# Weight tiles kept together on TensorE: k, r and v in groups of four tiles, and the decay's and a's products after the keys

## The chip, the cores and the metric

The kernel runs on one core of one Trainium2 chip. The metric is the device time of one execution in microseconds (us); lower is better. Before the change three runs took 1529.62, 1530.75 and 1531.14 us.

## The reference

One inference step of a decoder trunk with two layers, on 256 prompt tokens and 8 x 4 sample tokens (288 columns in all), everything in float32 with a model width of 1024. Cut to what matters:

```python
def trunk(x, p, ssm0, conv0, wkv0, shift0, prm):
    h = x
    for i in range(DEPTH):                      # 2 layers
        h = h + 0.5 * swiglu(rmsnorm(h, ...), ...)
        u = rmsnorm(h, ...)
        mix = mamba2_mixer(u, ...) if i % 2 == 0 else rwkv7_mixer(u, ...)
        h = h + mix
        h = h + 0.5 * swiglu(rmsnorm(h, ...), ...)
        h = h + (p[i] @ ple_in[i]) * sigmoid(rmsnorm(h, ...) @ ple_gate[i])
    return rmsnorm(h, norm_final), states

def rwkv7_mixer(u, S0, shift0, ...):
    # six mixtures of u with its predecessor: xr, xw, xk, xv, xa, xg
    r, k, v = xr @ w_r, xk @ w_k, xv @ w_v
    w = -softplus(-(w0 + tanh(xw @ w1) @ w2)) - 0.5          # the decay
    a = sigmoid(a0 + (xa @ a1) @ a2)
    g = sigmoid(xg @ g1) @ g2
    # per head of 64: kk = normalised k * k_k;  k = k * (1 + (a - 1) * k_a)
    # per token: S = S * exp(-exp(w)) - (S kk) (kk a)^T + v k^T ;  y = S r
    return (groupnorm(y) + bonus) * g @ w_o
```

## The kernel before, in words

All activations lie with features on the 128 partitions and the 288 tokens along the free dimension. A weight matrix is cut into tiles of 128 x 128. Most products run in three passes, so that a fast matmul format keeps float32 precision: a weight tile is split into a high part `whi` (by ScalarE, L57) and a low part `wlo` (by VectorE, L58), the activation is split in the same way, and `mm3` (L156) issues high x high, high x low and low x high into the same bank of PSUM. The key projection is the exception: it goes in plain float32 on the unsplit tile `raw` (`next_whole`, L71; the profile shows two matmul records for one such tile). Every matmul is issued by `mm` (L147), so most of them stand in the profile under line 149. Weight tiles come in the order of use from one packed stream (`Stream`, L28), eight tiles a transfer, split four tiles at a time.

The program is written with a tile framework that schedules when the kernel is built: it walks through the program with its own estimate of time, and whenever an engine is free it gives it, among the instructions whose inputs are ready, the one that comes first in program order. What it decides is then fixed: on the chip each engine runs its instructions strictly in that order and waits on semaphores. `high_priority()` is a block of the framework; instructions traced in it stand ahead of all others in this choice as soon as they are ready. `add_manual_dep` (in `after`, L127) fixes an order by hand; `mm` uses it only while `kept` is set, at the end of the RWKV stage.

The stages follow each other: feed-forward, Mamba, feed-forward, gated embedding, feed-forward, RWKV, feed-forward, gated embedding. The change concerns above all the RWKV stage (`rwkv`, L1516). It works on eight head pairs p = 0 to 7 of 128 features each. For a head pair there are three kinds of work:

- *bulk*: the projections. `bulk` (L1155) makes, for p > 0, first the products of the decay and of a (`small`, L1166: two matmuls each, then `sigmoid`, L1130, one VectorE and three ScalarE steps), then k (L1175), then r; `bulk2` (L1181) makes g and v. `proj` (L1138) takes eight weight tiles for k, r or v and yields after each. For p = 0 it also makes the mixtures of the activations (`mix`, L1115), and `small` comes after k.
- *prep* (L1234): from k, r, the decay and a of the head pair it makes the per-chunk matrices and inverts a triangular one by doubling; many matmuls on 64 x 64 quarters of the array, each followed by a ScalarE or VectorE step that the next one needs.
- *chain* (L1384): the recurrence over four chunks of 64 tokens and the samples: `solve`, `solved` and `state` for each chunk, again small matmuls with a step of another engine in between, then the group norm.

The loop at L1565 writes these in program order: in one round the chain of pair p-2, the second half of the preparation of p-1 and the first half of that of p advance by one step each, and then the bulk by 1.6 steps (`RATE`). `fill(p)` (L1545) says which bulk belongs to round p: g and v of p-1, then the decay, a, k and r of p+1. The banks of PSUM are dealt out in rings (L1527): the bulk has two in turn, the preparation three, the chain two and one for its outputs. `d["sw"]` and `d["sa"]` (the decay and a) have one buffer each, `d["k"]`, `d["r"]`, `d["v"]` and `d["g"]` two.

Of the kernel before, what the change touches and what calls it, by code (L numbers as in the profile page):

```python
# [1 line left out]

# [16 lines left out]
KD = 8  # L19
# [61 lines left out]
class K:  # L81
# [71 lines left out]
            self.kept = [i]  # L153
        return i

    def mm3(self, ps, w, x, start, stop):  # L156
        (wh, wl), (xh, xl) = w, x
        self.mm(ps, wh, xh, start=start, stop=False)
        self.mm(ps, wh, xl, start=False, stop=False)
        self.mm(ps, wl, xh, start=False, stop=stop)  # L160

    def hilo(self, hi, lo, src, scale=None):

# [686 lines left out]
def mamba(k, gain, g_next):  # L850
# [8 lines left out]

    with k.tc.tile_pool(name="mamba", bufs=1) as pool:  # L860
        pdt = proj("m_dt", 0)
        r = k.rstd()
        k.other = True
# [30 lines left out]
        for g in range(8):  # L894
            if g == 1:
                k.set_rings(main=[0, 1, 2], aux=[3, 4, 5, 6, 7])
            tiles = [("c", 16 + g), ("c", 24 + g), ("c", 2 * g), ("c", 2 * g + 1), ("z", 0), ("z", 1)]
            for n, (kind, i) in enumerate(tiles):
                if g == 0 and n == RAW:
                    k.flip()  # L900
                ps = proj("m_xbc" if kind == "c" else "m_z", i if kind == "c" else 2 * g + i)

                def evac(ps=ps, kind=kind, i=i, g=g, n=n, raw=g == 0 and n < RAW):
                    if kind == "c":
                        conv.setdefault(g, []).append(m.conv(g, n, i, ps, raw))
                    else:
                        t = m.t("z", bufs=3)
                        k.act(t, ps, AF.Copy)
                        zl.append((g, i, t))

                k.lag(evac)
                step()
                if n == 0 and g > 0:
                    boundary(g - 1)
                    gen = m.ssd(g - 1)
                if g == 0 and n in (0, 1):
                    next(dtg, None)
                if n > 0 and ahead is not None:
                    next(ahead, None)
                if g % 2 == 1 and g > 1 and n in (1, 2):  # L920
                    (m.norm_act, m.norm_dve)[n - 1](g - 2)
# [85 lines left out]
class Rwkv:  # L1007
# [130 lines left out]
    def proj(self, n, i, x, p):  # L1138

        k, d = self.k, self.d[p]  # L1140
        ps = k.bank("main")[:, :NT]
        for kt in range(KD):
            if p == 0:
                self.mix(i, kt, x)
            if n == "k":
                self.k.mm(ps, k.wn.next_whole("r_wk", kt, p), x[kt], start=kt == 0, stop=kt == KD - 1)
            else:
                k.mm3(ps, k.ws.next("r_w" + n, kt, p), x[kt], kt == 0, kt == KD - 1)
            if kt < KD - 1:
                yield  # L1150
        d[n] = self.t(n, bufs=2)
        k.act(d[n], ps, AF.Copy)
        yield

    def bulk(self, p):  # L1155

        nc, k = self.nc, self.k
        col = slice(p, p + 1)
        if p == 0:
            k.renew(0, 8, F32)  # L1160
            k.renew(8, 16)
            self.xk = k.A[0:8]
            self.xv, self.xr = [[None] * KD for _ in range(2)]
        d = self.d[p] = {}

        def small():  # L1166
            for n, x, b in (("sw", self.lw, "w0"), ("sa", self.la, "a0")):
                ps = k.bank("main")[:, :NT]
                self.stacked(ps, k.ws.next("r_" + n[1] + "2", 0, p), x)
                d[n] = self.t(n)  # L1170
                self.sigmoid(d[n], ps, k.g(b)[:, col])
            yield

        if p > 0:
            yield from small()  # L1175
        yield from self.proj("k", 2, self.xk, p)
        if p == 0:
            yield from small()
        yield from self.proj("r", 0, self.xr, p)

    def bulk2(self, p):  # L1181
# [334 lines left out]
def rwkv(k, g, g_next):  # L1516
# [3 lines left out]
    with k.tc.tile_pool(name="rwkv", bufs=1) as pool:  # L1520
# [44 lines left out]
        for p in range(KD + 2):  # L1565
            gens, acc = [], 0.0
            bulk = fill(p)
            if p > 1:
                gens.append(w.chain(p - 2))
            if 0 < p <= KD:  # L1570
                gens.append(preps.pop(p - 1))
            if p < KD:
                preps[p] = w.prep(p)
                gens.append(itertools.islice(preps[p], HALF))
            while gens:
                for q in list(gens):
                    if next(q, "end") == "end":
                        gens.remove(q)
                if w.last:
                    k.kept = k.kept or []  # L1580
                    acc += w.last.pop(0)
                else:
                    acc += RATE
                while acc >= 1:
                    acc -= 1
                    next(bulk, None)
            for _ in bulk:
                pass
# [198 lines left out]
```

## Time and profile before

| | us |
|---|---|
| median of three runs | 1530.75 |
| lowest and highest | 1529.62, 1531.14 |
| the profiled execution | 1529.38 |
| its span, first to last instruction | 1527.6 |
| one feed-forward stretch, 600 to 700 us: matmuls | 759 |
| RWKV's head pairs, 1003 to 1269 us: matmuls | 3971 |

How to read it: PE is TensorE's matmuls, PEld its weight loads, which overlap them; DVE is VectorE, ACT ScalarE, POOL GpSimd, SP the engine that issues the transfers. A line of the timeline gives start, length, engine, line, operation, what it writes and reads, the used part of the array (rows\*columns), the shape of the moving operand and how many of the kind stand together; a bracket at its end tells how long the engine was idle before it and who released it. A matmul's own length overlaps that of its neighbours, so differences of starts tell what it occupies. `bank<-act,whi` is a pass on the high part of a weight tile, `act,wlo` on the low part, `act,raw` the key projection, `lw` and `la` the products of the decay and a, `lgh`, `lgl` and `lg` those of g; names such as `X,N`, `Z,XT`, `rhs,TT` or `SAV,BKt` are the small matmuls of preparation and chain.

### The profile page before, as it was taken

What the parts mean: (1) busy time and instruction counts of PE and PEld (TensorE: products, weight loads), DVE (VectorE), ACT (ScalarE), POOL (GpSimd) and SP (SyncE); (2) the same over time, 40 slices, a digit from 0 to 9 for tenths busy, and PEclk for the clock granted to TensorE, in tenths of its full rate; (3) what the DMA queues carried; (4) which work ended last, traced back from release to release, by engine and by line L of the source; (5) the groups of instructions that cost most, each with busy time, mean ns of one, the idle gap of its engine ahead of it and who ended that gap; (6) DMA issues with size and microseconds to landing.
All of it is one profiled execution on the core that took longest, in us unless ns stands there. A gap on an engine that the chain in (4) does not pass through costs nothing.

```text
span 1527.6 us, 35589 instructions
## 1 busy us (share of the span) xinstructions
PE 1504.1 (98%) x14178; PEld 1418.5 (93%) x14178; DVE 1099.2 (72%) x2320; ACT 966.1 (63%) x2201; POOL 60.2 (4%) x162
## 2 busy tenths in 40 slices
PE   9999999999999999999999999999999999999997
PEld 9999998999999999999999999777777778999997
DVE  7666578899998666656876655897777768666666
ACT  6555458999997655554755554586666646555545
POOL 0000002112110000000000000200000000000000
PEclk9999999999999999999999999999999999999999
DMA  7555564766766555555555555622221125555552
GB/s 233 166 167 165 167 204 138 241 235 214 240 220 195 174 167 167 165 169 166 170 166 166 166 166 166 208 84 73 71 85 58 62 75 165 167 167 166 166 169 68
DMA packets 75575, 243.48 MB, mean 159 GB/s; under 512 B 11728, under 2 KB 16976, under 8 KB 75408
## 3 DMA queue, kind: packets, MB, share of 16 engines
q1 hardware_dynamic: 75408, 241.21, 49.1%
q8 instruction: 111, 1.82, 0.5%
q14 instruction: 56, 0.46, 0.1%
HBM read 226.54 MB, written 14.64 MB: 158 GB/s over the span
## 4 chain that ended last, share of the span: by engine, by line
PE 91%; DVE 4%; ACT 3%; DMA 1%; issue 1%; SPq 0%; DVEq 0%; ACTq 0%
PE bank L149 85%; PE bank L783 1%; DVE wlo L58 1%; PE bank L787 1%; PE bank L779 1%; DMA raw<-in_wn 1%; ACT whi L57 1%; PE bank L760 0%; DVE AA L1288 0%; ACT L136 0%; PE bank L818 0%; ACT seg L141 0%; DMA raw<-in_w 0%; PE bank L752 0%; ACT xc L141 0%
## 5 line engine op out<-in xcount | busy, mean ns | idle before, releaser
L149 PE MATMUL bank<-act,whi 128*128 128x288 f32 x5520 | 1121.7, 297 | 2.5 <-ACT whi L57 1.6
L149 PEld LDWEIGHTS bank<-act,whi 128*128 128x128 f32 x5520 | 885.7, 188 | 11.0 <-ACT whi L57 2.1
L149 PE MATMUL bank<-act,wlo 128*128 128x288 f32 x2760 | 812.4, 295 | 0.1
L57 ACT ACTIVATE whi<-raw 128x512 fp32r<-128x512 f32 x754 | 473.5, 632 | 445.6 <-PE bank L149 435.3
L58 DVE TENSOR_TENSOR wlo<-raw,whi 128x512 fp32r<-128x512 f32 x754 | 515.8, 689 | 270.2 <-ACT whi L57 241.9
L149 PEld LDWEIGHTS bank<-act,wlo 128*128 128x128 f32 x2760 | 520.4, 189 | 1.9 <-DVE wlo L58 0.3
L149 PE MATMUL bank<-more,whi 128*128 128x288 f32 x384 | 77.1, 295 | 0.0
L149 PEld LDWEIGHTS bank<-more,whi 128*128 128x128 f32 x384 | 61.4, 188 | 0.0
L149 PE MATMUL bank<-act,raw 128*128 128x288 f32 x176 | 54.0, 429 | 2.7 <-DVE sw L1133 1.4
L335 DVE TENSOR_TENSOR u<-bank,s 128x288 f32<-128x288 f32 x88 | 40.2, 456 | 22.8 <-PE bank L149 22.8
L149 PE MATMUL bank<-more,wlo 128*128 128x288 f32 x192 | 56.4, 294 | 0.0
L332 DVE TENSOR_TENSOR t<-bank,rstd 128x288 f32<-128x288 f32 x88 | 39.8, 456 | 22.2 <-PE bank L149 22.1
L684 DVE SCALAR_TENSOR_TENSOR conv_a<-X,vec,conv_a 128x312 f32<-128x312 f32 x96 | 51.0, 535 | 2.4 <-ACT conv_a L141 2.1
L141 ACT ACTIVATE s<-t 128x288 f32<-128x288 f32 x104 | 45.8, 443 | 6.1 <-DVE t L377 4.4
L141 ACT ACTIVATE X<-bank 128x256 f32<-128x256 f32 (+2 forms) x98 | 30.6, 343 | 16.9 <-PE bank L149 16.2
L149 PEld LDWEIGHTS bank<-act,raw 128*128 128x128 f32 x176 | 29.9, 189 | 11.2 <-DVE sw L1133 1.7
L141 ACT ACTIVATE act<-h,vec 128x288 fp32r<-128x288 f32 (+1 forms) x71 | 37.0, 527 | 4.1 <-DMA h<-in_xT 2.9
L149 PEld LDWEIGHTS bank<-more,wlo 128*128 128x128 f32 x192 | 36.2, 189 | 0.0
L136 ACT ACT_TABLE_LOAD x25 | 32.1, 1283 | 1.1 <-PEq L1761 0.7
L170 DVE SCALAR_TENSOR_TENSOR act<-h,vec,act 128x288 fp32r<-128x288 f32 x56 | 28.3, 512 | 5.6 <-ACT act L141 5.6
L181 DVE TENSOR_TENSOR ss<-ss,sq 128x288 f32<-128x288 f32 x62 | 28.0, 452 | 1.9 <-ACT sq L141 1.7
L141 ACT ACTIVATE sq<-h 128x288 f32<-128x288 f32 x63 | 26.9, 431 | 3.8 <-DVE h L381 3.7
(371 smaller groups left out, 1605.4 us busy)
## 6 DMA issues: line engine op xcount, KB each, us to landing
raw<-in_w SPq DMA_DIRECT2D x377, 512.0 KB, 3.6
h0a<-in_ssm_a SPq DMA_DIRECT2D x16, 512.0 KB, 5.8
h0b<-in_ssm_b SPq DMA_DIRECT2D x16, 512.0 KB, 5.4
out_ssm_s<-h0b SPq DMA_DIRECT2D x16, 512.0 KB, 4.4
raw<-in_wn SPq DMA_DIRECT2D x11, 512.0 KB, 4.2
S<-in_wkv_in SPq DMA_DIRECT2D x8, 256.0 KB, 3.0
out_wkv_s<-S SPq DMA_DIRECT2D x8, 256.0 KB, 2.1
h<-in_xT SPq DMA_DIRECT2D x8, 144.0 KB, 4.5
```

Of the source, the lines that this page charges most:

```text
L57: nc.scalar.activation(hi, src, AF.Copy)
L58: nc.vector.tensor_tensor(lo, src, hi.bitcast(F32), ALU.subtract)
L136: load = self.nc.scalar.preload_act_table_set(s)
L141: i = self.nc.scalar.activation(out, in_, func, **kw)
L149: i = self.nc.tensor.matmul(*a, **kw)
L170: nc.vector.scalar_tensor_tensor(lo, src, scale, hi.bitcast(F32), ALU.mult, ALU.subtract)
L181: nc.vector.tensor_tensor(self.ss, self.ss, sq, ALU.add)
L332: nc.vector.tensor_tensor(t, pg, r, ALU.mult)
L335: nc.vector.tensor_tensor(u, pu, s, ALU.mult)
L684: nc.vector.scalar_tensor_tensor(a[:, :312], X[:, t:t + 312], k.g(f"conv_w{t}")[:, ct:ct + 1], a[:, :312], ALU.mult, ALU.add)
L779: nc.tensor.matmul(pyi[q:q + 32, 128 + 4 * b:132 + 4 * b], h0a[:, b, q:q + 32], C[:, 256 + 4 * b:260 + 4 * b], start=True, stop=True)
L783: nc.tensor.matmul(py[64 * hh:64 * hh + 64, o:o + n], xdt[:n, c, 2 * j + hh], Pm[:n, hh, o:o + n], start=True, stop=True)
```

## The change

In `mm3` the second and the third pass of every weight tile are traced in a `high_priority()` block, in all stages; the first pass too where the new argument `follow` is set. `proj` sets it for k, r and v of every head pair but the first, for all tiles but the first and the fifth, and for k it puts its float32 matmul in the same block. So from the first pass of tile 0 or 4 on, the passes of four tiles are the scheduler's first choice one after the other. In `bulk` the products of the decay and a now follow the keys for every head pair, as they did before for the first alone. No instruction is added or dropped.

```diff
+    def together(self, follow):
+
+        return self.tc.high_priority() if follow else contextlib.nullcontext()
+
-    def mm3(self, ps, w, x, start, stop):
+    def mm3(self, ps, w, x, start, stop, follow=False):
         (wh, wl), (xh, xl) = w, x
-        self.mm(ps, wh, xh, start=start, stop=False)
-        self.mm(ps, wh, xl, start=False, stop=False)
-        self.mm(ps, wl, xh, start=False, stop=stop)
+        with self.together(follow):
+            self.mm(ps, wh, xh, start=start, stop=False)
+        with self.together(True):
+            self.mm(ps, wh, xl, start=False, stop=False)
+            self.mm(ps, wl, xh, start=False, stop=stop)
...
             if n == "k":
-                self.k.mm(ps, k.wn.next_whole("r_wk", kt, p), x[kt], start=kt == 0, stop=kt == KD - 1)
+                with k.together(p > 0 and kt % 4 > 0):
+                    self.k.mm(ps, k.wn.next_whole("r_wk", kt, p), x[kt], start=kt == 0, stop=kt == KD - 1)
             else:
-                k.mm3(ps, k.ws.next("r_w" + n, kt, p), x[kt], kt == 0, kt == KD - 1)
+                k.mm3(ps, k.ws.next("r_w" + n, kt, p), x[kt], kt == 0, kt == KD - 1, p > 0 and kt % 4 > 0)
...
-        if p > 0:
-            yield from small()
         yield from self.proj("k", 2, self.xk, p)
-        if p == 0:
-            yield from small()
+        yield from small()
         yield from self.proj("r", 0, self.xr, p)
```

More of the change, by code (lines that the diff above doesn't have):

```diff
@@ L1 @@
+import contextlib
 import itertools
```

## The prediction

> **What bounds the kernel now.** I read the page first, then the busy time of the engines by stretches, then TensorE's timeline inside one stretch.
>
> ```profile
> span 1527.6 us, 35589 instructions
> ...
> PE 1504.1 (98%) x14178; PEld 1418.5 (93%) x14178; DVE 1099.2 (72%) x2320; ACT 966.1 (63%) x2201; POOL 60.2 (4%) x162
> ...
> PE 91%; DVE 4%; ACT 3%; DMA 1%; issue 1%; SPq 0%; DVEq 0%; ACTq 0%
> ```
>
> TensorE is busy for 98% of the span and carries 91% of the chain that ended last. So time can be won only by making TensorE's own sequence shorter, and lost only by putting holes into it. The next view shows what a matmul costs in two stretches.
>
> ```profile
> core 0: us, PE busy (x) PEld busy (x) DVE busy (x) ACT busy (x) POOL busy (x), PEclk, DMA share, GB/s
> 600.00:700.00 100.00, 100.00 (x759) 100.00 (x758) 60.26 (x104) 53.03 (x96) 0.00 (x0) 1.00 0.51 165
> 1102.81:1134.48 31.67, 31.34 (x491) 23.64 (x490) 23.49 (x66) 21.47 (x60) 0.00 (x0) 1.00 0.26 78
> ```
>
> In a feed-forward stretch, 759 matmuls of one shape follow each other in 100 us: 0.132 us each. Nothing stands between them, so the first edit (second and third pass at the first choice) finds nothing to reorder there. In the RWKV stage one head pair takes 31.67 us, a period that recurs from pair to pair, with 491 matmuls of many shapes. TensorE is idle for only 0.33 us of it by this row, yet the matmuls on weight tiles (three passes for each of v's and r's 16 tiles, two records for each of k's 8) are a small part of it. The timeline shows what else fills it.
>
> ```profile
> 1103.93 0.53 PE L149 MATMUL bank<-act,whi 128*128 128x288 f32 x2
> ...
> 1104.96 0.29 PE L149 MATMUL bank<-act,wlo 128*128 128x288 f32 x1
> 1105.18 0.31 PE L149 MATMUL bank<-X,N 64*64 64x64 f16 x8
> 1105.42 0.53 PE L149 MATMUL bank<-act,whi 128*128 128x288 f32 x2
> 1105.80 0.29 PE L149 MATMUL bank<-act,wlo 128*128 128x288 f32 x1
> ...
> 1107.64 0.40 PE L149 MATMUL bank<-act,whi 128*128 128x288 f32 x1
> ...
> 1114.71 0.75 PE L149 MATMUL bank<-act,raw 128*128 128x288 f32 x2
> ...
> 1120.50 0.34 PE L149 MATMUL bank<-Z,XT 64*64 64x64 f16 x10
> 1120.68 0.32 PE L149 MATMUL bank<-XT,Z 64*64 64x64 f16 x10
> ...
> 1125.74 1.24 PE L149 MATMUL bank<-act,raw 128*128 128x288 f32 x4
> ...
> 1127.17 0.54 PE L149 MATMUL bank<-act,whi 128*128 128x288 f32 x2
> ...
> 1129.11 0.55 PE L149 MATMUL bank<-act,whi 128*128 128x288 f32 x2
> ...
> 1134.11 0.40 PE L149 MATMUL bank<-qh,ones_m 128*128 128x288 f32 x1
> ```
>
> Matmuls on the full array (128\*128) alternate with groups on a quarter of it (64\*64). Each way there and back costs something. From the last full one (1104.96) to the first small one (1105.18) pass 0.22 us, 0.09 more than its 0.132. The eight small ones take 0.24 us until the next full one (1105.42); ten of their kind in the middle of small work take 0.18 us (1120.50 to 1120.68), so eight should take 0.14, and 0.10 is the way out. The two full ones then take 0.38 us (1105.42 to 1105.80) for 0.264: another 0.12. **One visit to the small work costs 0.09 + 0.10 + 0.12 = 0.30 us beyond its arithmetic.** In the period I count 17 returns to full-array work, the first at 1103.93, the last at 1134.11: four inside v's eight tiles (1103.93 to 1107.64), two for the products of the decay and a, six inside k's (1114.71 to 1125.74), three inside r's (1127.17 to 1129.11), and two where the full-size matmuls on the ones matrix stand. That is some 5 us of 31.67: the switching, not the waiting, is what there is to win.
>
> **The change, part by part.** No instruction is added or removed; the same work gets another order, chosen when the kernel is built.
>
> *k, r and v keep four tiles together (from the second head pair on).* Eight tiles can then be entered at two places, the first and the fifth tile. Per period k goes from six returns to two, v from four to two, r from three to two: seven fewer. The code makes these groups for seven head pairs, so 49 fewer. I assume that small groups which no longer find a gap join the next ones, and that changing between small kinds is as cheap as the two rows at 1120.50 make it look.
>
> *Second and third pass at the first choice, everywhere.* In RWKV's remaining three-pass work (the output projection, the gate) this can join a few split triples; I take three returns fewer. In the Mamba stage it moves a visit by at most two matmuls without removing it: nothing. In the feed-forward stages, by the row with 759, nothing. What hides it there is that a later pass was next in order anyway; if that were wrong, a change of order among equal matmuls of 0.132 us still costs nothing, and the end of an accumulation moves by a few tenths of a us.
>
> The price of one return is bounded by 0.21 us (the late starts on both sides alone, 0.09 + 0.12) and by 0.45 us (from 1104.96 to 1105.80 pass 0.84 us, less three times 0.132, as if the small ones were free in company). I take 0.30, since it has a rate for the small ones from their own kind. 52 returns fewer give 52 x 0.30 = **15.6 us less**.
>
> ```profile
> 1105.42 0.30 PEld L149 LDWEIGHTS bank<-act,whi 128*128 128x128 f32 x2
> ```
>
> The weight load of the first full matmul begins at 1105.42, with the matmul itself and after the small ones, so the way back is not hidden. [...]
>
> *What the grouping takes away.* Small steps depend on each other through ScalarE or VectorE, and full-array work covers that latency. What an uncovered step costs is seen where the stage runs out of cover, at its end:
>
> ```profile
> PE bank L149 <- DVE SAV L1432: 1.0, 2, 0.5
> PE bank L149 <- DVE rhs L1426: 0.6, 1, 0.6
> PE bank L149 <- ACT ch L141: 0.6, 1, 0.6
> ```
>
> 2.2 us in four waits: 0.55 us each. What is queued behind such a wait is everything on TensorE, which runs in order; then the ScalarE and VectorE steps of the other head pairs. A group of four tiles is 12 x 0.132 = 1.6 us, long enough to cover such a latency for all three streams of small work (the chain of one head pair, two halves of preparation), but there are fewer groups. The number of new stalls lies between none and one for each return removed. From 1120.50 to 1125.74 the small work already runs 5.2 us without any weight tile, while the period's row leaves 0.33 us idle in all. So I am near the lower end: one a period, 7 x 0.55 = **3.9 us more**.
>
> *The decay's and a's products after the keys.*
>
> ```profile
> 1110.53 0.52 DVE L1133 TENSOR_SCALAR sw<-bank,vec 128x288 f32<-128x288 f32 x1
> ...
> 1114.12 0.75 DVE L1248 TENSOR_TENSOR_SCAN rs_y<-scan,sw 128x288 f32<-128x288 f32 x1
> ...
> 1127.02 0.41 ACT L141 ACTIVATE k<-bank 128x288 f32<-128x288 f32 x1 [2.01 <-PE bank L149]
> ```
>
> Four matmuls, two VectorE reads of the banks and six ScalarE steps move behind k's eight tiles; no DMA of theirs moves alone, the weight stream is packed in the new order. Two banks serve all these products in turn. Before, k's bank is the one that the decay's product gives back with the read at 1110.53, and k begins at 1114.71; after, k follows v's products at once, and r waits for that read. The scan at 1114.12 needs the decay and would start some 4 us later, but the same preparation needs k, which lands at 1127.02, later than the scan by 13 us. So the move hides behind k: nothing. If the cover failed, one stall of 0.55 us a period, 3.9 us, would be added; if k's earlier start fills the gap of small work before 1114.71, about as much is saved. Both ends go into the range.
>
> **Sum.** The profiled execution took 1529.38 us, of which 1527.6 are the span; the median of the three runs, 1530.75, is 1.37 above it. 1529.38 - 15.6 + 3.9 = 1517.7, and with 1.37 added **1519 us**. Its own range: at best 52 x 0.45 = 23.4 less without stalls, 1507; at worst 52 x 0.21 = 10.9 less and two stalls a period (7.7), 1527.5.
>
> **The rivals.**
>
> *The cover is lost (slower).* Place: the small steps between two groups in RWKV. Price 0.55 us a stall. From 28 stalls in the stage on (15.6 / 0.55), four a period, nothing is won; with six a period 42 x 0.55 = 23.1, less 15.6, the time is 1538; with one for each return removed 28.6 - 15.6 = 13 more, 1544. For it: there are far more small steps than the eight to ten groups of a period that would be left. Against it: the stretch of 5.2 us above, and three independent streams. Chance 0.13.
>
> *The clock drops (no change).*
>
> ```profile
> 1223.94:1227.36 3.42, 3.42 (x64) 2.64 (x64) 0.91 (x4) 2.00 (x6) 0.00 (x0) 1.00 0.58 205
> 1227.36:1230.77 3.41, 3.41 (x39) 2.74 (x41) 1.71 (x5) 1.66 (x4) 0.00 (x0) 0.50 0.00 0
> ```
>
> For 3.41 us the granted clock is 0.50, once in this stage, right after a stretch in which small matmuls dominate. Grouping makes such stretches longer. One drop costs at most half of 3.41, 1.7 us; one in each of seven periods takes 11.9 us, all of the gain: 1531. [...] Against the rival: the period above, with its 5.2 us without a weight tile, kept a clock of 1.00. Chance 0.07.
>
> *The order hardly changes, or the way back is cheap.* If the scheduler finds the small steps ready at the same places, or if a weight load pulled ahead leaves only the 0.09 us of the way in (52 x 0.09 = 4.7, less 3.9), the time is 1530. [...] Together 0.06.
>
> *More joins than I count.* If the products of the decay and a and those on the ones matrix join too, nine fewer a period, 66 in all, and no stall comes, 66 x 0.30 = 20 us: 1511, and with the high price 1501. Chance 0.12.
>
> **How the numbers follow.** The forecast has 0.62. About 0.2%, 3 us, is what a measurement of this kernel can tell from no change. Faster: 0.62 + 0.12 = 0.74. Same: 0.07 + 0.06 = 0.13. Slower: 0.13. The range reaches from 1503, inside the case of more joins, to 1535, which takes in no change and the light end of the lost cover.
>
> **What would show it.** Right: in the RWKV stage fewer returns a period (about ten), runs of 12 passes for v and r and of eight records for k, a period near 30 us, the other stages at the same length. Wrong: runs as long as planned but with idle time before the small matmuls, put down to VectorE or ScalarE (lost cover); a granted clock below 1.00 from 1003 to 1269 us (clock); the same 17 returns (no new order); or another price of a return, when the period shortens by much more or less than 0.30 us for each one gone.

## The result and the profile after

The changed kernel takes **1548.34 us** (median of four runs, 1545.34 to 1549.52); the kernel before, in four runs beside it, 1530.86 (1529.62 to 1531.14). The ratio is 1.0113, 95% interval 1.0095 to 1.0130: 17.5 us slower where 12 us faster was forecast. The profiled execution took 1547.74 us.

First the page of the kernel after:

```profile
span 1546.0 us, 35594 instructions
...
PE 1506.6 (97%) x14178; PEld 1431.2 (93%) x14178; DVE 1101.7 (71%) x2320; ACT 967.8 (63%) x2201; POOL 60.4 (4%) x162
...
PEclk9999999999999999999999999989999979999999
...
PE 87%; ACT 5%; DVE 5%; issue 1%; DMA 1%; POOL 0%; SPq 0%; DVEq 0%; ACTq 0%; POOLq 0%
```

The same 14178 matmuls keep TensorE busy for about as long as before. But its share of the chain that ended last fell from 91% to 87%, and two slices of the granted clock show less than full speed. Both lie in the RWKV stage. Outside it little moved, as the busy time by stretches says, first of the kernel after, then of the kernel before (0 to 520 us and 520 to 940 us; then the rest behind the RWKV stage):

```profile
0.00:520.00 520.00, 515.82 (x4821) 501.12 (x4822) 405.24 (x854) 377.58 (x941) 49.80 (x124) 1.00 0.61 199
520.00:940.00 420.00, 420.00 (x3171) 419.44 (x3170) 274.60 (x494) 232.32 (x424) 0.00 (x0) 1.00 0.53 167
1287.30:1546.00 258.70, 250.24 (x1890) 249.24 (x1889) 172.88 (x324) 143.13 (x265) 0.00 (x0) 0.99 0.50 154
```

```profile
0.00:520.00 520.00, 515.72 (x4812) 500.19 (x4813) 405.35 (x853) 376.43 (x940) 49.45 (x124) 1.00 0.61 198
520.00:940.00 420.00, 420.00 (x3169) 419.29 (x3168) 274.57 (x494) 232.74 (x424) 0.00 (x0) 1.00 0.52 166
1269.20:1527.60 258.40, 250.32 (x1890) 249.22 (x1889) 172.95 (x324) 143.35 (x265) 0.00 (x0) 0.99 0.48 155
```

Behind the RWKV stage the length is the same to 0.3 us. Ahead of it the changed kernel is a little faster: by 940 us it has done eleven matmuls more, and it reaches the first key weight tile of the RWKV stage 1.5 us earlier (before, then after):

```profile
969.60 0.99 PE L149 MATMUL bank<-act,raw 128*128 128x288 f32 x3 [0.40 <-ACT pin L141]
```

```profile
968.10 0.99 PE L150 MATMUL bank<-act,raw 128*128 128x288 f32 x3 [0.69 <-ACT pin L142]
```

About 1 us of this is won in the Mamba stage and belongs to the first edit: the five kernels below that have it in all stages start this tile at 968.1 to 968.8 us, the kernel before and the three that leave the other stages alone at 969.2 to 969.6. The last `cl,ones_m` stands at 1269.2 before and at 1287.3 after, 18.1 us later; from the first key tile on, the RWKV stage is 19.6 us longer. I cut it from 1003 us on into a front (up to the first `ch,center`, the first group norm), a middle of four periods, and an end. Kernel before, then after:

```profile
1003.00:1066.50 63.50, 62.13 (x990) 48.05 (x989) 50.34 (x135) 47.29 (x127) 0.00 (x0) 1.00 0.24 80
1066.50:1192.50 126.00, 124.72 (x1959) 94.38 (x1957) 95.39 (x265) 87.33 (x241) 0.00 (x0) 1.00 0.23 70
1192.50:1269.20 76.70, 72.64 (x1029) 57.17 (x1028) 52.52 (x143) 39.24 (x108) 0.00 (x0) 0.98 0.24 76
```

```profile
1003.00:1077.70 74.70, 69.88 (x1033) 55.88 (x1032) 53.96 (x138) 48.72 (x132) 0.00 (x0) 0.91 0.25 75
1077.70:1207.60 129.90, 123.33 (x1968) 100.17 (x1968) 97.89 (x269) 89.54 (x242) 0.00 (x0) 0.93 0.21 65
1207.60:1287.30 79.70, 67.49 (x950) 53.39 (x949) 48.33 (x133) 35.61 (x98) 0.00 (x0) 0.87 0.20 64
```

Each part is longer: 11.2, 3.9 and 3.0 us. (The parts do not hold quite the same work: the front has 43 matmuls more than before, the end 79 fewer.) The column behind the busy times of the five engines is the granted clock: 1.00, 1.00 and 0.98 before; 0.91, 0.93 and 0.87 after. In the trace that is 15 windows of 3.41 us at clock 0.50, in nine drops of one to three windows (3.41, 6.83 or 10.24 us), against one. It is no accident of one execution: the mean granted clock was 0.981 to 0.983 in all four runs of the changed kernel, and 0.989 to 0.998 in the 54 runs of the kernel before that stand beside the experiments. And TensorE waits where it did not. Its waits from 1003 to 1285 us after (engine, line, waited for; total us, times, longest us):

```profile
PE bank L150 <- DVE rstd L1514: 2.5, 3, 1.3
PE bank L150 <- DVE AA L1293: 2.0, 3, 0.7
PE bank L150 <- ACT g L142: 1.9, 2, 1.5
PE bank L150 <- ACT SAV L142: 1.7, 5, 0.4
PE bank L150 <- DVE Z L1348: 1.6, 4, 0.5
...
PE bank L150 <- DVE sw L1140: 0.6, 2, 0.4
```

Before, this list had eight entries, the longest of 1.2 us in all. Now there are 21, nearly all of them steps of the preparation and of the chain (`rstd`, `AA`, `SAV`, `Z`). The moved decay (`sw`) is a small one.

What both do together is seen in TensorE's timeline of the kernel after, at a run of weight tiles in the third period:

```profile
1142.33 0.40 PE L150 MATMUL bank<-cl,center 128*128 128x288 f32 x1 [0.27 <-DVE cl L1500]
...
1144.51 0.85 PE L150 MATMUL bank<-act,whi 128*128 128x288 f32 x2 [0.42 <-DVE sw L1140]
1145.16 0.44 PE L150 MATMUL bank<-act,wlo 128*128 128x288 f32 x1
...
1145.88 0.44 PE L150 MATMUL bank<-act,wlo 128*128 128x288 f32 x1
...
1147.56 0.44 PE L150 MATMUL bank<-cl,ones_m 128*128 128x288 f32 x1
```

The run is what was planned, twelve passes in one go. But ahead of it TensorE stood still for 0.27 and for 0.42 us, and the run falls into a half-clock window (from 1144.5 to 1147.9): three passes take 0.72 us (1145.16 to 1145.88) instead of 0.40, the twelve 3.05 us (1144.51 to 1147.56) instead of 1.6.

**The books of the stage.** For every kernel I took four sums from its trace, from 1000 us to the last `cl,ones_m`: the length; the returns from small to full-array work, counted as in the prediction; the waits, that is, time in which no matmul record runs; and the work that was done in half-clock windows, each record counted at its cost at full clock. That cost is 0.134 us for a full one (90 in 12.05 us, in p_clock below). For the others it is my estimate by their columns: 64/288 x 0.134 = 0.030 us for 64, half of that where two halves of the array alternate (in p_clock float16 matmuls with 64 columns start 0.016 us apart so), twice for a record in float32 (in the kernel before four records of `act,raw` with 288 columns take 1.17 us, from 1125.74 to the next matmul at 1126.91). The twelve passes above took 1.9 times their 1.6 us at half clock; taking twice, I let this sum stand for the most that the lower clock has cost. The length is counted from 1000 us, not from the same instruction; where that matters it is said below.

| kernel | length | returns | waits | work at half clock |
|---|---|---|---|---|
| before | 269.2 | 156 | 7.3 | 1.5 |
| after | 287.3 | 106 | 23.8 | 21.1 |
| e1_triples_only | 271.1 | 138 | 8.5 | 6.4 |
| e2_order_only | 283.2 | 155 | 11.9 | 11.0 |
| g_small_before | 285.1 | 114 | 22.4 | 23.7 |
| g_mid | 286.5 | 122 | 19.8 | 17.7 |
| g_pairs | 279.6 | 131 | 16.6 | 13.3 |
| h_triples_mid | 266.7 | 145 | 6.3 | 0.9 |
| h_pairs_mid | 267.4 | 136 | 7.9 | 2.6 |
| h_fours_mid | 275.2 | 132 | 13.3 | 12.6 |
| e4_before_f32 | 306.8 | 138 | 6.0 | 0.9 |
| e3_after_f32 | 312.1 | 102 | 12.1 | 3.9 |

From before to after: 50 returns x 0.30 = 15.0 us less, 16.5 us more waits, at most 19.6 us more by the clock; together 21.1, measured 18.1 (19.6 from the first key tile on). By this count the gain came as forecast, and waits and clock each took about as much back.

What the clock really cost can be estimated from runs of one kernel, whose order is fixed while the granted clock differs from execution to execution. Of the kernel before, one run took 1529.67 us at a mean clock of 0.998 and one 1538.57 us at 0.989. One window at half clock lowers the mean by 0.5 x 3.41 / 1530 = 0.0011, so eight windows lie between the two: 1.1 us each. A line through all 54 runs gives 1.0 us a window. That is less than the 1.4 us of work in a window of the changed kernel (21.1 / 15); perhaps part of the slower work falls into time in which TensorE would have waited anyway, but no run tests that. At 1.0 us, the 14 windows more cost about 14 us instead of 19.6, and the sum becomes 15.5.

### The profile page after: what moved, and what is told of

Same layout as the page of the kernel before. It is cut to its first block, busy times and chain, and to the rows that moved or that the text cites. A ratio compares the mean times of both kernels' runs of the same rounds, so it can differ in the third digit from the quotient of the medians.

```text
span 1546.0 us, 35594 instructions
## 1 busy us (share of the span) xinstructions
PE 1506.6 (97%) x14178; PEld 1431.2 (93%) x14178; DVE 1101.7 (71%) x2320; ACT 967.8 (63%) x2201; POOL 60.4 (4%) x162
## 4 chain that ended last, share of the span: by engine, by line
PE 87%; ACT 5%; DVE 5%; issue 1%; DMA 1%; POOL 0%; SPq 0%; DVEq 0%; ACTq 0%; POOLq 0%
PE bank L150 82%; DVE wlo L59 1%; PE bank L790 1%; ACT whi L58 1%; PE bank L786 1%; PE bank L794 1%; ACT seg L142 1%; DMA raw<-in_w 1%; PE bank L767 0%; ACT s L142 0%; PE bank L759 0%; ACT act L142 0%; DVE act L174 0%; DMA raw<-in_wn 0%; DMA spill<-pin 0%
## 5 line engine op out<-in xcount | busy, mean ns | idle before, releaser
L150 PE MATMUL bank<-act,raw 128*128 128x288 f32 x176 | 48.5, 424 | 2.8 <-ACT g L142 1.5
```

The costliest lines, as they stand in the source:

```text
L150: i = self.nc.tensor.matmul(*a, **kw)
```

## The experiments

Two theories stood at first. *Stalls*: longer runs of small work uncover dependent steps, and TensorE waits. *Clock*: small matmuls in longer clumps halve the clock by themselves, without any wait. The first four runs take the change apart and change the small matmuls.

**e1_triples_only**: the second and third pass alone at the first choice; no groups, products ahead of the keys.

```diff
-                with k.together(p > 0 and kt % 4 > 0):
+                with k.together(False):
...
-                k.mm3(ps, ..., x[kt], kt == 0, kt == KD - 1, p > 0 and kt % 4 > 0)
+                k.mm3(ps, ..., x[kt], kt == 0, kt == KD - 1, False)
...
+        if p > 0:
+            yield from small()
         yield from self.proj("k", 2, self.xk, p)
-        yield from small()
+        if p == 0:
+            yield from small()
```

> Only the first edit: second and third pass of every weight tile at the first choice; no group of four, the products of the decay and a back ahead of the keys. Theory (the groups of four bundle the small work, which loses its cover and lets the clock drop): few returns go, so 1526 to 1533 us, at most three half-clock windows of 3.41 us in the RWKV stage. Rival (the first choice itself costs, in any stage): clearly above 1535 us.

Measured 1531.09 us against 1531.11, ratio 1.0001 (0.9990 to 1.0012): no difference. Its three parts show why:

```profile
1003.00:1066.00 63.00, 61.79 (x992) 47.69 (x992) 49.71 (x131) 45.72 (x124) 0.00 (x0) 1.00 0.26 81
1066.00:1189.90 123.90, 123.29 (x1961) 95.37 (x1960) 95.13 (x265) 88.11 (x241) 0.00 (x0) 1.00 0.23 71
1189.90:1271.10 81.20, 74.88 (x1024) 59.12 (x1023) 52.81 (x143) 39.38 (x108) 0.00 (x0) 0.92 0.22 71
```

The middle is 2.1 us shorter than before (eight returns fewer there), the end 4.5 us longer, at a clock of 0.92, with four half-clock windows where the theory allowed three in the whole stage. So this edit is no source of the loss in the steady periods; it gains there and about 1 us in the Mamba stage, and loses as much where the RWKV stage ends.

**e2_order_only**: the kernel before, with `small()` behind the keys for every pair.

```diff
-        if p > 0:
-            yield from small()
         yield from self.proj("k", 2, self.xk, p)
-        if p == 0:
-            yield from small()
+        yield from small()
```

> Only the third edit: the products of the decay and a follow the keys for every head pair, no first choice anywhere. Theory (groups of four): within 4 us of before, 1527 to 1535 us, clock as before. Rival (the late decay and a delay the next head pair's preparation): 1538 us or more, with TensorE idle ahead of preparation's matmuls.

Measured 1536.36 us (1532.66 to 1544.08), ratio 1.0035 (1.0018 to 1.0053): about 5 us slower, between what the theory and the rival expected. The move is not free. The middle kept its length, front and end did not (this profiled execution, at 1544.08, is the longest of its runs, so the amounts are on the high side; it ran 10.24 us of the Mamba stage at half clock and reaches the first key tile 3.7 us later than the kernel before, so 3.0 of the front's 6.7 us are the stage's own):

```profile
1003.00:1073.20 70.20, 65.59 (x1013) 50.48 (x1012) 53.90 (x141) 50.29 (x134) 0.00 (x0) 0.98 0.24 74
1073.20:1199.70 126.50, 123.96 (x1948) 93.58 (x1948) 96.98 (x266) 87.68 (x243) 0.00 (x0) 1.00 0.22 69
1199.70:1283.20 83.50, 78.97 (x1018) 62.42 (x1017) 52.36 (x142) 39.14 (x107) 0.00 (x0) 0.86 0.22 69
```

**e4_before_f32 and e3_after_f32**: both kernels with the matmuls of the triangular inversion in float32 instead of float16 (and one buffer fewer in the rings of raw and of split weight pieces, to make room), which makes the small work longer and leaves the order's logic alone.

```diff
-F16 = mybir.dt.float16
+F16 = mybir.dt.float32
```

> The kernel before with the same edit: inversion in float32, one weight buffer of each kind less. It is the partner of the changed kernel with that edit. Both theories: some us slower than before through longer matmuls and VectorE steps, 1530 to 1550 us, with one half-clock window or none in the RWKV stage.

> [...] Clock theory (the array idles inside clumps of short matmuls, so the clock is halved): the half-clock windows in the RWKV stage fall from fifteen to five or fewer and the gap between the two kernels shrinks from 17 us to 6 or less. Stall theory alone (lost cover): the gap stays at 12 to 20 us whatever the clock does.

Measured 1569.62 us (ratio to the kernel before 1.0251, 1.0236 to 1.0266) and 1573.45 us (1.0278, 1.0259 to 1.0296). Both are far longer than the 1530 to 1550 us expected of the first: a small matmul in float32 took 0.059 us in p_clock below (240 in 14.15 us), one in float16 0.016. The difference between the two orders shrinks from 17.5 to 3.8 us. Half-clock windows in the stage: one against four; before, one against fifteen. That spoke for the clock, but the waits shrank as well (6.1 us more instead of 16.5), so the two theories were not yet told apart. By the books the changed order should even have won 1.7 us here where it lost 5.3: for this pair 7 us are not accounted for.

**p_clock**: matmuls in a fixed order, placed behind the last stage of the kernel before.

```diff
+        full(90)
+        for _ in range(10):
+            full(12)
+            small(40, H16, "half")
+        full(90)
+        for _ in range(40):
+            full(3)
+            small(10, H16, "half")
+        full(90)
+        small(900, H16, "half")
+        full(90)
+        small(240, G, "single")
+        full(90)
+        # ten times: full(12), then four groups of ten small,
+        # three of them waiting for a VectorE step on the group before
```

> The kernel before, with a series of matmuls added behind its last stage, in a fixed order and without any wait but in the last part; its output is the same, only the added work makes it longer. Between the parts stand 90 full-array matmuls (128x128, 288 columns, 11.9 us). Parts: (1) ten times 12 full and 40 small ones (64x64, float16); (2) the same matmuls as forty times 3 full and 10 small; (3) 900 small ones on end; (4) 240 small ones in float32; (5) ten times 12 full and four groups of 10 small, each group waiting for a VectorE step on the group before. By 0.132 us a full and 0.018 us a small one, part 1 is 10 x (1.58 + 0.72) = 23 us plus 10 x 0.30, part 2 the same plus 40 x 0.30 = 12 us, so part 2 should be 9 us longer than part 1 if a return costs 0.30 us. Theory of the clock (clumped small work halves the granted clock, without any wait): windows of 0.50 in part 1 and in part 3, none in part 2. Theory of the stalls (the clock falls because TensorE waits): clock 1.00 in parts 1 to 3, windows of 0.50 in part 5 alone. If none of the five parts shows a drop, the clock answers to something else than the kind and grouping of the matmuls.

The five parts, without the 90 full ones between them:

```profile
1544.15:1567.69 23.54, 23.54 (x510) 21.66 (x509) 0.00 (x0) 0.00 (x0) 0.00 (x0) 1.00 0.01 3
1580.46:1614.53 34.07, 34.07 (x518) 26.05 (x518) 0.00 (x0) 0.00 (x0) 0.00 (x0) 1.00 0.01 1
```

```profile
1626.58:1649.97 23.39, 15.48 (x901) 14.77 (x901) 0.00 (x0) 0.00 (x0) 0.00 (x0) 1.00 0.02 5
1662.02:1676.17 14.15, 14.15 (x482) 14.08 (x481) 0.00 (x0) 0.00 (x0) 0.00 (x0) 1.00 0.02 5
1688.29:1730.00 41.71, 32.00 (x530) 26.64 (x530) 6.75 (x30) 0.00 (x0) 0.00 (x0) 1.00 0.01 2
```

Two answers. *The price of a return is right.* The first two rows hold the same 400 small matmuls, and 108 against 117 full ones: 34.07 - 23.54 - 9 x 0.134 = 9.3 us for 30 more returns, 0.31 us each. *Both theories of the clock fall.* 900 small matmuls on end, 23 us without a full one, leave it at 1.00; so do ten rounds with three waits of half a us each. In these parts neither small matmuls nor short waits lowered the clock. (The 900 did not run evenly: after the first 153 and then after every 128 TensorE stood still for more than 1 us.)

What does? For all 925 windows of 3.41 us at full clock in the RWKV stage of the twelve kernels (all but the two with added matmuls) I set the work in each, by the costs above, against the clock that the trace shows in the window behind it:

| share of work in the window | windows | followed by half clock |
|---|---|---|
| under 0.39 | 34 | 32 |
| 0.39 to 0.47 | 21 | 4 |
| over 0.47 | 870 | 2 |

In the kernel before one window lies under 0.39, in the changed one eight. The count has exceptions: two windows with a share of 0.74 (e1, at 1258.5 us) and 0.91 (e3, at 1300.3 us) were followed by half clock too, and the share gives no reason for them. This is not the busy time of the profile. The window before one of the drops of the kernel after, and the drop:

```profile
1110.40:1113.80 3.40, 2.61 (x45) 1.73 (x43) 2.88 (x10) 3.07 (x8) 0.00 (x0) 1.00 0.35 82
1113.80:1117.20 3.40, 3.28 (x19) 2.94 (x20) 2.95 (x11) 3.05 (x8) 0.00 (x0) 0.50 0.00 0
```

TensorE counts as busy for 2.61 of 3.40 us here, since each record counts in full (0.31 us for the `X,N` at 1113.40, whose like start 0.016 us apart in p_clock); by the costs above the work is 0.21 of the window. That gave a third theory, *the share*: waits and thin work pull the share of a window down, and the window behind it runs at half clock. p_share sets it against waits alone and against the kind of matmul.

**p_share**: small or full matmuls in groups, each group waiting for a VectorE step on the one before.

```diff
+        for s in (8, 12, 16, 20, 24, 28):
+            m = H16
+            for j in range(24):
+                ps = small(s, m, "turn")
+                ...
+                nc.vector.tensor_scalar(m, ps[:, 0:64], 1.0, -1.0, ALU.min, ALU.max)
+            full(90)
+        for n in (3, 4, 5, 6, 7):
+            ...
+                for _ in range(n):
+                    k.mm(ps, W, x, start=True, stop=True)
+                ...
+                nc.vector.tensor_scalar(x, ps, 1.0, -1.0, ALU.min, ALU.max)
```

> The kernel before, with a second series of matmuls behind its last stage in a fixed order (its output is the same, only the added work makes it longer): what share of its time TensorE must work to keep its clock. Six parts of 24 groups of s small matmuls (64x64, float16; s = 8, 12, 16, 20, 24, 28), each group waiting for a VectorE step on the group before; then five parts of 14 groups of n full-array matmuls (n = 3 to 7), each waiting for a VectorE step of full width; 90 full ones between any two parts. By 0.019 us a small one, 0.134 us a full one and the 0.51 us of a wait in the first series, the shares of work are about 0.23, 0.31, 0.37, 0.43, 0.47, 0.51 for the small ones, and from some 0.3 to 0.55 for the full ones (their wait has no row yet). Theory of the share (a window of 3.41 us in which TensorE works for less than about 0.41 of the time at full speed is followed by one at half clock, whatever the kind of matmul): half-clock windows in the parts under 0.40, none in those over 0.45, for small and full ones alike. Rival (only waits count, not the share): all eleven parts drop, since each waits as often. Rival (the kind counts): the small parts drop at every share, the full ones at none.

The parts with s = 8, 24 and 28, then those with n = 3 to 7:

```profile
1546.60:1563.50 16.90, 9.46 (x194) 6.41 (x193) 5.17 (x23) 0.00 (x0) 0.00 (x0) 0.61 0.00 1
...
1683.50:1706.70 23.20, 15.78 (x577) 13.00 (x576) 5.17 (x23) 0.00 (x0) 0.00 (x0) 0.80 0.01 3
1720.70:1749.60 28.90, 21.46 (x673) 18.41 (x672) 5.17 (x23) 0.00 (x0) 0.00 (x0) 0.57 0.01 3
1763.70:1781.30 17.60, 11.01 (x36) 7.32 (x36) 5.50 (x12) 0.00 (x0) 0.00 (x0) 0.65 0.00 1
1797.00:1818.50 21.50, 14.90 (x49) 10.96 (x49) 5.49 (x12) 0.00 (x0) 0.00 (x0) 0.56 0.00 1
1834.60:1857.40 22.80, 16.20 (x61) 12.49 (x61) 5.50 (x12) 0.00 (x0) 0.00 (x0) 0.63 0.00 0
1873.20:1892.50 19.30, 12.70 (x73) 9.88 (x73) 5.50 (x12) 0.00 (x0) 0.00 (x0) 1.00 0.00 0
1906.90:1927.70 20.80, 14.24 (x84) 11.45 (x84) 5.50 (x12) 0.00 (x0) 0.00 (x0) 1.00 0.00 1
```

By the starts, a small one takes 0.016 us in these groups and a round at full clock 0.63 us (s = 8) to 0.95 (s = 28), 1.21 (n = 3) to 1.74 (n = 7). So the shares of work are 0.20, 0.28, 0.34, 0.39, 0.43 and 0.47 for the small ones; all six dropped, but that with 0.43 held full clock for 13.7 us first. (The one with 0.47 dropped behind a window that caught only 88 of its matmuls, 88 x 0.016 / 3.41 = 0.41.) For the full ones they are 0.33, 0.40, 0.45, 0.50 and 0.54: the first three dropped, the last two did not. Between the parts that dropped and those that did not lies a share near 0.45 for both kinds here, a little over the 0.41 expected; no sharp bound was seen, since the part with 0.43 kept full clock behind two windows that hold 96 of its matmuls each and dropped behind the next, which holds 96 too, and 17 of the 21 windows between 0.39 and 0.47 in the table kept it. That waits alone decide, or the kind alone, is excluded by the last two rows and the first three of the full ones. A part that had dropped stayed low (s = 24 at 0.50 from 1697.2 us to its end at 1706.7, n = 5 from 1840.5 to 1857.4): a round of s = 28 then took 1.28 us for the same 0.45 us of work, 0.35, and full clock came back only with the 90 full ones behind it.

The remaining runs ask which part of the change pulls the share down, and where.

**g_small_before**: the changed kernel with the products back ahead of the keys (the last part of the diff of e1 alone).

> The changed kernel with the products of the decay and a put back ahead of the keys; later passes first and groups of four stay. Against the triples alone (1531) it adds the groups alone, against the changed kernel (1548) it takes the move alone. If the three parts simply add up, the move gives back its own 5 us and the time is 1543 (1.008). Theory of the clock: half-clock windows stay at ten or more in the RWKV stage (the clumps are the same), 1540 to 1546. Theory that the move is what uncovers the steps (the products no longer stand as cover ahead of k): idle time falls from 23.5 to under 12 us and the time to under 1537.

Measured 1546.58 us, ratio 1.0106 (1.0091 to 1.0121), not to be told from the changed kernel's 1.0113. Waits stayed at 22.4 us and half-clock windows at 15. The theory that the move uncovers the steps falls: the groups do nearly all of it, and the move's own 5 us do not add up with them.

**g_mid**: the groups for the pairs 1 to 5 only.

```diff
-                with k.together(p > 0 and kt % 4 > 0):
+                with k.together(0 < p < 6 and kt % 4 > 0):
```

(and the same condition in the call of `mm3`)

> The changed kernel with the groups of four for the head pairs 1 to 5 only: the last two head pairs, whose weight tiles are the cover of the stage's end, stay as before; the move of the products and the first choice of later passes stay everywhere. If the loss sits at the end of the stage, where the weight tiles ran out 19 us before the small work did, the time falls to the level of the move alone, 1535 to 1538, with the long stretch without a weight tile gone. If it is spread over the periods (clumps that halve the clock, waits between them), only two sevenths of it go: 1543 to 1545.

Measured 1547.54 us, ratio 1.0113 (1.0095 to 1.0132): nothing is won by sparing the last two pairs, less than either expectation. By the books it brings 16 returns back (4.8 us) and takes 4.0 us of waits and 3.4 us of work at half clock away: what the groups of these two pairs win and lose nearly cancels, and the loss does not sit in their weight tiles alone.

**g_pairs**: groups of two tiles (`kt % 2 > 0` in place of `kt % 4 > 0`).

> The changed kernel with groups of two tiles instead of four for k, r and v; all else as changed. Returns: k 4 a period, v and r 4 each at most, so about 14 to 16 a period, nearer to the 17 of before than to the 10 of the change. Theory of the clock and of the stalls alike: shorter clumps, fewer half-clock windows (about 8 instead of 15) and less idle time (about 13 us), the time near that of the move alone, 1536 to 1541. If the loss came from the move and the first choice of later passes, and not from the groups, it stays near 1546.

Measured 1541.71 us, ratio 1.0073 (1.0056 to 1.0090), just above what was expected, with 10 half-clock windows and 16.6 us of waits where 8 and 13 were expected. Front, middle and end:

```profile
1003.00:1074.40 71.40, 67.82 (x995) 53.41 (x995) 51.57 (x134) 46.34 (x125) 0.00 (x0) 0.88 0.21 67
1074.40:1198.60 124.20, 120.54 (x1950) 93.49 (x1948) 96.13 (x265) 87.99 (x242) 0.00 (x0) 1.00 0.21 70
1198.60:1279.60 81.00, 72.55 (x1014) 58.00 (x1014) 52.20 (x142) 38.80 (x106) 0.00 (x0) 0.89 0.23 72
```

The middle is 1.8 us shorter than before, at a clock of 1.00; front and end lose 7.9 and 4.3 us, at 0.88 and 0.89. So small groups of tiles paid in the middle, where all three streams of small work run. That front and end lose because the first and the last pair have too little beside them is argued, not shown: this run has the move of the products in it too.

**h_triples_mid**: e1 reduced to the calls for v and r from the second pair on; output projection, gate and the other stages as before.

```diff
-        with self.together(True):
+        with self.together(later):
...
-                k.mm3(ps, ..., x[kt], kt == 0, kt == KD - 1, p > 0 and kt % 4 > 0)
+                k.mm3(ps, ..., x[kt], kt == 0, kt == KD - 1, False, p > 0)
```

(no `together` for k, and `small()` ahead of the keys)

> The kernel before, with the second and third pass at the first choice for v and r from the second head pair on and nowhere else (no groups, the products ahead of the keys, the output projection and the gate as before): what is left of the change where it neither uncovers steps nor touches the stage's end. In the run of the later passes alone the four middle periods were 2.1 us shorter than before and the end 4.5 us longer, with 12.6 us at half clock. If that loss came from the output projection's passes, it goes: 1528 to 1529 (0.9985). If it came from weight tiles used up earlier by v and r, it stays: 1531.

Measured **1527.13 us** against 1532.35, ratio 0.9967 (0.9955 to 0.9979): faster than both kernels. The clock does not explain this: at the same mean clock of 0.997 its runs took 1526.5 to 1527.1 us, those of the kernel before 1529.1 to 1531.9.

```profile
1003.00:1066.90 63.90, 62.76 (x997) 48.64 (x996) 50.89 (x135) 46.91 (x127) 0.00 (x0) 1.00 0.26 80
1066.90:1190.80 123.90, 123.28 (x1961) 95.37 (x1960) 95.11 (x265) 88.05 (x240) 0.00 (x0) 1.00 0.24 71
1190.80:1266.70 75.90, 71.78 (x1024) 56.41 (x1023) 52.67 (x143) 39.08 (x108) 0.00 (x0) 1.00 0.25 76
```

The middle keeps e1's gain, and the end loses nothing: in the RWKV stage the two kernels differ behind the first pair only by the joined passes of the output projection and the gate, so these are what e1 lost there: 5 us between the two profiled executions, 4 us between the medians.

**h_pairs_mid**: that one, with k in groups of two for the pairs 2 to 5 (`with k.together(1 < p < 6 and kt % 2 > 0)`).

> The one above, and k in groups of two tiles for the head pairs 2 to 5 only. It takes about two returns a period more away, 8 x 0.30 = 2.4 us. If the four middle periods keep their work share over 0.41 in every window (with groups of two everywhere they had no half-clock window and were 1.8 us shorter than before) and the end stays as before, the time is 1526 to 1528. If the cover that k gives the preparation is used up at the end of the stage, it is 1530 or more, with half-clock windows behind 1220 us.

Measured 1528.82 us, ratio 0.9969 (0.9956 to 0.9983): faster than before, if 0.8 us over what was hoped for, and not to be told from h_triples_mid. In the profiled execution nine more returns are gone (136 instead of 145), and 1.6 us of waits and one more half-clock window took their place.

**h_fours_mid**: h_triples_mid with groups of four for k, v and r, for the pairs 2 to 5 (`1 < p < 6 and kt % 4 > 0`).

> As the triples of v and r alone (1527, products ahead of the keys, output projection as before), with groups of four tiles for k, v and r added for the head pairs 2 to 5 only, where the steady periods are. It takes about 25 returns away there, 25 x 0.30 = 7.5 us. If four tiles together are bad only at the stage's two ends, the time is 1520 to 1523. If they also uncover dependent steps in the steady periods, waits of TensorE grow by 5 us or more there and windows with a work share under about 0.43 are followed by half clock: 1528 to 1537, that is nothing won or a loss, with the half-clock windows between 1070 and 1200 us.

Measured 1537.07 us, ratio 1.0033 (1.0017 to 1.0048): slower. The middle:

```profile
1071.50:1198.00 126.50, 119.38 (x1892) 93.05 (x1892) 92.95 (x258) 84.34 (x233) 0.00 (x0) 0.92 0.19 62
```

18 returns fewer than before (52 instead of 70), yet 7.1 us of waits instead of 1.3, and six half-clock windows where there was none. So four tiles together lose in the steady periods too, and not only at the stage's ends.

## Why the prediction was wrong

*The returns: right.* 52 fewer were forecast, 51 were counted (154 before, 103 after, from 1003 us on), ten a period as announced, in runs of twelve passes. The price of 0.30 us was confirmed by itself: 0.31. That a weight load pulled ahead leaves only 0.09 us of it, as the rival with 0.06 supposes, no run shows.

*The stalls: the step that failed.* The prediction put it: "So I am near the lower end: one a period, 7 x 0.55 = 3.9 us more." It was 16.5 us, 30 stalls' worth. The ground for the low end was one stretch of 5.2 us without a weight tile in which TensorE hardly waited. But that stretch is not thin work: by the costs above, its 122 small matmuls fill 0.96 of it, four with 512 columns alone nearly 2 us (0.95 us for the two at 1122.88, 1.00 us for the two at 1124.36). It could not show what happens where the small steps have nothing ready; the groups bring such places about, as the list of 21 waits and the middle of h_fours_mid show. And a single steady period was read for the whole stage: by the rows above, waits grew by 5.3 us in the four middle periods, by 3.4 in the front, and by 8.2 at the end.

*The clock: the second size that failed.* The rival had its mechanism nearly right, "at most half of 3.41, 1.7 us" for a drop and one drop a period. There were nine drops instead of seven, and they lasted 15 windows, each with 1.4 us of work (21.1 / 15), some 1.0 us of time by the line through the runs: about 14 us in place of nothing in the forecast's sum. Its "for it" named the wrong cause, stretches in which small matmuls dominate; its "against it" was again the 5.2 us at clock 1.00, which with 0.96 of work belongs to the row over 0.47 of the table, where 2 of 870 windows were followed by half clock. The row that decided stood in the prediction: 3.42 of 3.42 us busy, then 0.50. By the costs above the work in that window is 0.38. Long idle times were not needed: the 15 windows at 0.50 stand in a stage whose longest wait is 1.5 us.

*The rivals were treated as alternatives, and both came.* Waits alone would have eaten the gain (15.0 against 16.5) and left about 1532; the clock alone would have taken some 14 us, at most 19.6. As far as the share explains the drops, they are one event: the waits, together with thin small work, pulled windows under 0.39 (eight in the changed kernel, one before), and the work behind them was done at a clock of 0.50. A case with both was not among the priced ones.

*The products behind the keys: wrong by 5 us when made alone* (1.0035), near the bound of 3.9 that the prediction gave for a failed cover. But the waits there are not on `sw` (0.6 us, in e2_order_only as in the changed kernel); the loss stood in the front and in the end, not once a period. Much of it came with the clock: at a mean clock of 0.995 the run of e2_order_only took 1533.48 us, those of the kernel before 1532.0 to 1533.4, and its median is 5 us longer because most of its runs had a lower clock than that. Which of the steps behind the later decay brings this about was not settled. Beside the groups it was no longer measurable.

*The passes elsewhere: right for the feed-forward stages* (759 matmuls in 100 us left nothing to reorder, and the stages behind RWKV kept their length to 0.3 us). In the Mamba stage, where the prediction said nothing would change, they won about 1 us. "Three returns fewer" in RWKV's remaining three-pass work hid a loss: joined passes of the output projection and the gate cost the end of e1 some 5 us (81.2 against 75.9 in h_triples_mid).

What stays open: with the whole work at half clock as the clock's price, the books miss the measured length by 7 us for the float32 pair and by 9 us for g_small_before, and come within 4 us for the other eight kernels. At 1.0 us a window the 9 us go: 42 returns fewer (12.6), 15.1 us more waits and 14 windows more make 16.5 us, measured 15.9; the other eight stay within 4 us. The 7 us of the float32 pair stay.

## What to carry to other kernels

Price a saving on a busy engine together with the cover that it uses up: interleaved work that looks like costly switching may be what fills the waits, so join only what the steps beside it don't need (here the three passes of one tile, -0.3%, and not four tiles, +1.1%). Judge the cover at the thinnest part of a stage, its beginning and its end, not in one steady period. And where a trace shows the granted clock drop, count the work in each window by what the matmuls cost back to back, not by the profile's busy time: here 32 of 34 windows of 3.41 us with a share under 0.39 were followed by one at half clock, each worth about 1.0 us, so that a wait there most likely cost more than its own length. Whether another kernel has the same share, no run shows.

## What the runs showed of the hardware

In p_share the granted clock went with the share of work, for 64x64 float16 and for full-array matmuls alike: the parts of small ones with shares of 0.20 to 0.47 (by that estimate of the work) and those of full ones with 0.33 to 0.45 dropped to mean clocks of 0.56 to 0.80, the full ones with 0.50 and 0.54 kept 1.00. In the RWKV stage of the twelve kernels 32 of 34 windows of 3.41 us under 0.39 were followed by half clock, 4 of 21 between 0.39 and 0.47, and 2 of 870 over that. The busy time did not show it: in the kernel before a window with TensorE busy for 3.42 of 3.42 us was followed by half clock, while in p_clock 900 small matmuls on end, busy for 15.48 of 23.39 us, kept 1.00.

A window at half clock cost about 1.0 us of time, an estimate from the 54 runs of the kernel before: with one fixed order they range from 1529.1 us at a mean clock of 0.997 to 1538.6 at 0.989.

Small matmuls (64x64 float16, alternating over two halves of the array) started 0.016 us apart on average, whether 28 stood behind a wait (p_share), 40 behind full-array work or 128 in a row (both p_clock). But there 900 on end took 23.39 us, 0.026 each, since TensorE paused six times, after the first 153 and then after every 128:

```profile
PE bank L149 <- issue: 7.9, 6, 1.5
q8 instruction: 7, 0.11, 2.0%
```

The first line says that in six pauses it stood still for 7.9 us without waiting for anything that the profile shows; the second, that 7 packets (0.11 MB) came through the queue for instructions between 1626 and 1650 us. The pauses may be waits for instructions (7 packets beside six pauses); no run tests that.
